# State space branch of a two-block transformer: a group's turning moved behind the norm of the group before, its features ahead of that group's second part

## The chip, the cores and the metric

The kernel runs on one core of one Trainium2 chip. The metric is the device time of one execution in microseconds (us), less is better. Engines: PE is TensorE (matmuls and transposes), PEld its weight loads, DVE is VectorE, ACT is ScalarE, POOL is GpSimd, SP is SyncE, whose queue loads the weights.

## The reference, cut to what matters

Two transformer blocks, D = 1024, 512 tokens, batch 1. The change lies in the state space branch of the second block: `proj` is the normed hidden state times `w_in`; 2048 columns `z` are the gate, 4096 columns `xbc` the features, 64 the time steps. There are 8 groups of 4 heads (head width 64), a state of 128 and 4 chunks of 128 tokens.

```python
def ssd_branch(z, xbc, dt_raw, conv_w, conv_b, dt_bias, a_log, d_skip, norm_g):
    xbc = silu(depthwise_conv_centred(xbc, conv_w, conv_b))     # 5 taps along the tokens
    xs, Bm, Cm = xbc[..., :2048], xbc[..., 2048:3072], xbc[..., 3072:]
    dt = softplus(dt_raw + dt_bias); A = -exp(a_log)
    y = ssd_chunked(xs, dt_fwd, A[0], Bm, Cm) + flip(ssd_chunked(flipped, A[1])) + d_skip * xs
    y = y * silu(z)
    yg = y.reshape(b, l, 8, 256)                                # one row per group
    return (yg * rsqrt(mean(yg * yg) + EPS)) * norm_g

def ssd_chunked(x, dt, A, Bm, Cm):          # per chunk of 128 tokens, r = 4 heads of a group
    CB = einsum(Cc, Bc);  Wd = CB * segsum_exp(dt * A)
    y_diag = einsum(Wd, x * dt)
    states = einsum(Bc, decay_states, x * dt);  prev = scan(carry * decay + states)
    return y_diag + einsum(Cc, prev, exp(a_cs))
```

Behind it `ssd @ w_ssd_branch` is summed into an accumulator.

## The kernel before, in words

Every large product is three fp32r matmuls per 128 rows of the inner dimension (`mm3`, L457 to L459: high part times high, high times low, low times high), each 128x128 by 128x512. Weights come by the SP queue into `raw` and are split into the two parts `hl` by ACT (L165) and DVE (L167). PSUM has 8 banks of 128x512: three for tiles `psm` (large products) and five for tiles `pss` (everything small).

The state space stage takes about 1313 to 1800 us of the span. A group g has these parts, methods of `Group`:
- `feats` (L1273): four `psm` tiles of 24 matmuls each (two of x features, one of B, one of C), with channels on the partitions. Each is evacuated by `conv` (L1251): ACT L1253 (centre tap), four DVE passes L1257 that read the same PSUM bank, ACT L1259 (silu). It writes `xs` (buffer "xsT", two tiles, that is one group's), `Bf` and `Cf` (two each, two groups').
- `gate` (L1286): for even g the gate's columns of two groups, four `psm` tiles, ACT L1292.
- `turn` (L1294): per chunk three transposes on PE (L1302 twice, L1303) into a `pss` bank, ACT L1304 and L1305 copy it to `x` and `Bt`. It is the last reader of `xs`, so the conv of the next group's features cannot write before it.
- `first` (L1335): PE L1343 C times B, DVE L1346 its diagonal; the steps of the states (`step`: DVE L1310, PE L1312, then ACT L1315 or DVE L1319); `decays` per chunk (POOL's DMA L1327 from `aD`, DVE L1329 and L1330, ACT L1332, DVE L1333).
- `second` (L1359): per chunk PE L1368/L1370 and L1381, DVE L1371, L1375, L1376, L1382, L1383, ACT L1384 (sum of squares).
- `third` (L1386): the norm. DVE L510, POOL L506 (power), DVE L1392 on four chunks, eight PE transposes L1394, then the split ACT L468 and DVE L469 into the operand of the output product.
- `ssd_out` (L1398, two groups) and `ssd_out_group` (L1402): the output product, DVE L625.

The framework's scheduler lists the instructions by their place in the program and by when its own simulation has them ready; on the chip every engine then runs its list in that fixed order. The loop at L1417 is what it gets.

Of the kernel before, what the change touches and what calls it, by code (L numbers as in the profile page):

```python
# [246 lines left out]
def body(ctx, tc, I, out, dbg=None, stop=None):  # L247
# [12 lines left out]
    def PM():  # L260
        return ps_m.tile([P, 512], F32, tag="m", name="psm")
# [185 lines left out]
    def uk(k):  # L447
        if k < 4:
            return UAh[:, k], UAl[:, k]
        return st["UBh"][:, k - 4], st["UBl"][:, k - 4]  # L450
# [4 lines left out]
    def mm3(ps, a, b, first, last, partial=False):  # L455

        nc.tensor.matmul(ps, a[0], b[0], start=first, stop=False, skip_group_check=partial)  # L457
        nc.tensor.matmul(ps, a[0], b[1], start=False, stop=False, skip_group_check=partial)  # L458
        nc.tensor.matmul(ps, a[1], b[0], start=False, stop=last, skip_group_check=partial)  # L459
# [137 lines left out]
    def tok2(w, src, evac, n_k=8):  # L597

        for t in range(NT):
            ps = PM()  # L600
            tk = slice(t * P, (t + 1) * P)
            for k in range(n_k):
                xh, xl = src(k)
                mm3(ps, (xh[:, tk], xl[:, tk]), w[k], k == 0, k == n_k - 1)
            evac(t, ps)
# [15 lines left out]
    def add_to(dst, ps, first):  # L621
        if first:
            nc.scalar.activation(out=dst, in_=ps, func=AF.Copy)
        else:
            nc.vector.tensor_tensor(out=dst, in0=ps, in1=dst, op=ALU.add)  # L625
# [334 lines left out]
    for j in range(4):  # L960
        heads = []
        for hh in range(2):
            hd = 2 * j + hh
            Z = wk.get("Z", 1024, 4)
            G = wk.get("G", 512, 4)
# [432 lines left out]
    def ssd_out(i):  # L1398
        for u in range(2):
            tok2(WT.get(f"so{i}{u}"), uk, lambda t, ps: add_to(acc[:, t, u * 512:(u + 1) * 512], ps, i == 0), n_k=4)  # L1400

    def ssd_out_group(g):  # L1402
        for u in range(2):
            w = WT.get(f"so3{g}{u}")
            for t in range(NT):
                ps = PM()
                tk = slice(t * P, (t + 1) * P)
                for k in range(2):
                    uh, ul = uk((2 * g + k) % 4)
                    mm3(ps, (uh[:, tk], ul[:, tk]), w[k], k == 0, k == 1)  # L1410
                add_to(acc[:, t, u * 512:(u + 1) * 512], ps, False)

    G = [Group(g) for g in range(8)]
# [3 lines left out]
    for g in range(8):  # L1417
        G[g].first()
        G[g].gate()
        G[g].second()  # L1420
        if g < 7:
            G[g + 1].feats()
        else:
            ssd_out_group(6)
        if g in (2, 4, 6):
            ssd_out(g // 2 - 1)
        if g < 7:
            G[g + 1].turn()
        G[g].third()
    ssd_out_group(7)  # L1430
    for t in range(NT):
        nc.gpsimd.dma_start(h[:, t], hD[t * P:(t + 1) * P, :])
# [238 lines left out]
def kernel_body(tc, I, out, dbg=None, stop=None):  # L1671
    with ExitStack() as ctx:
        body(ctx, tc, I, out, dbg, stop)
# [25 lines left out]
```

## Time and profile before

| | |
|---|---|
| three runs | 2581.29, 2582.27, 2585.32 us; median 2582.27 |
| profiled execution | 2581.83 us, span 2580.1 us |
| busy, share of the span | PE 97%, PEld 81%, DVE 66%, ACT 47%, POOL 7% |
| granted clock of PE, mean | 0.989 |
| HBM | 109 GB/s over the span |

The span is what the profiler recorded from the first to the last instruction; 1.7 us lie around it. A line such as `1425.25 0.66 PE L1394 MATMUL pss<-ident,h ... x2 [4.51 <-DVE h L1392]` of a timeline reads: at 1425.25 us PE began two matmuls of line 1394 that took 0.66 us; before it PE had been idle for 4.51 us, which DVE's line 1392 ended by writing `h`.

### The profile page before, as it was taken

The numbers are of one execution on the slowest core, as the hardware profiler recorded it, in microseconds if no ns is written. First come the engines' busy times: TensorE is split into PE (matmuls) and PEld (weight loads), VectorE is DVE, ScalarE is ACT, GpSimd is POOL, SyncE is SP. The second block draws the span as 40 slices with busy tenths as digits, with TensorE's granted clock in tenths as the row PEclk, the third lists the DMA queues.
The fourth block names the chain that finished last, engine by engine and source line by source line (L and its number), as shares of the span: only waits on it lengthen the run. The fifth ranks groups of instructions, "written<-read, shape, count | busy, mean of one in ns | idle before, by whom it ended". The sixth has DMA issues, their size and how long they took to land. (4 is left out here: it accounts for less than half of the span.)

```text
span 2580.1 us, 33650 instructions
## 1 busy us (share of the span) xinstructions
PE 2504.9 (97%) x12848; PEld 2088.2 (81%) x12848; DVE 1714.5 (66%) x3048; ACT 1220.2 (47%) x2181; POOL 183.5 (7%) x199
## 2 busy tenths in 40 slices
PE   8999999999999989999999999998999999999998
PEld 7888888778888768877888788787887789878877
DVE  5566567775566657577477788887555466487674
ACT  6333345443476554444356554563455436444342
POOL 1100220000201030000121100010000000100000
PEclk9999999999999989999999999998999999999999
DMA  5521235333232133453334333352221233243441
GB/s 175 162 66 61 87 115 169 125 108 129 82 96 89 63 97 113 140 179 98 102 109 125 106 104 109 104 148 77 73 67 40 84 113 123 82 147 104 141 139 58
DMA packets 202001, 278.11 MB, mean 108 GB/s; under 512 B 10800, under 2 KB 127776, under 8 KB 201840
## 3 DMA queue, kind: packets, MB, share of 16 engines
q1 hardware_dynamic: 190352, 236.29, 29.4%
q0 software_dynamic: 10192, 34.96, 5.0%
q10 hardware_dynamic: 1296, 4.72, 0.5%
q8 instruction: 101, 1.65, 0.3%
q14 instruction: 60, 0.49, 0.1%
HBM read 271.56 MB, written 9.61 MB: 109 GB/s over the span
## 5 line engine op out<-in xcount | busy, mean ns | idle before, releaser
L458 PE MATMUL psm<-XTl,hl 128*128 128x512 f32 (+1 forms) x1400 | 537.3, 384 | 7.8 <-DVE XTl L466 7.8
L457 PE MATMUL psm<-XTh,hl 128*128 128x512 f32 (+1 forms) x1400 | 534.5, 382 | 5.9 <-ACT XTh L465 5.1
L459 PE MATMUL psm<-XTh,hl 128*128 128x512 f32 (+1 forms) x1400 | 533.3, 382 | 0.0
L165 ACT ACTIVATE hl<-raw 128x1024 fp32r<-128x1024 f32 x303 | 319.3, 1056 | 313.9 <-PE psm L459 132.6
L167 DVE TENSOR_TENSOR hl<-raw,hl 128x1024 fp32r<-128x1024 f32 x287 | 352.7, 1233 | 149.0 <-ACT hl L165 147.9
L458 PEld LDWEIGHTS psm<-XTl,hl 128*128 128x128 f32 x1400 | 266.3, 190 | 56.9 <-DVE XTl L466 8.6
L457 PEld LDWEIGHTS psm<-XTh,hl 128*128 128x128 f32 x1400 | 265.9, 190 | 55.7 <-ACT XTh L465 6.1
L459 PEld LDWEIGHTS psm<-XTh,hl 128*128 128x128 f32 x1400 | 266.3, 190 | 48.5
L457 PE MATMUL psm<-hl,XTh 128*128 128x512 f32 (+1 forms) x640 | 231.1, 362 | 4.4 <-ACT XTh L465 3.3
L458 PE MATMUL psm<-hl,XTh 128*128 128x512 f32 (+1 forms) x640 | 229.9, 359 | 0.1
L459 PE MATMUL psm<-hl,XTl 128*128 128x512 f32 (+1 forms) x640 | 229.1, 358 | 0.0
L457 PE MATMUL psm<-hl,UAh 128*128 128x512 f32 x368 | 148.6, 405 | 4.9 <-DVE ACC L625 1.5
L458 PE MATMUL psm<-hl,UAh 128*128 128x512 f32 x368 | 144.9, 395 | 0.0
L459 PE MATMUL psm<-hl,UAl 128*128 128x512 f32 x368 | 143.7, 396 | 0.0
L457 PEld LDWEIGHTS psm<-hl,XTh 128*128 128x128 f32 x640 | 122.3, 191 | 21.8 <-ACT XTh L465 3.7
L458 PEld LDWEIGHTS psm<-hl,XTh 128*128 128x128 f32 x640 | 122.2, 191 | 16.6 <-issue 0.5
L459 PEld LDWEIGHTS psm<-hl,XTl 128*128 128x128 f32 x640 | 122.3, 191 | 15.9 <-issue 0.5
L671 ACT ACTIVATE WK<-psm 128x512 f32<-128x512 f32 x66 | 39.5, 598 | 160.8 <-PE psm L459 160.8
L457 PE MATMUL psm<-hl,UBh 128*128 128x512 f32 (+1 forms) x240 | 93.5, 391 | 1.1 <-ACT UBh L468 0.8
L459 PE MATMUL psm<-hl,UBl 128*128 128x512 f32 (+1 forms) x248 | 94.3, 388 | 0.0
L1257 DVE SCALAR_TENSOR_TENSOR WS<-psm,CW,WS 128x511 f32<-128x511 f32 (+1 forms) x120 | 87.5, 740 | 8.7 <-ACT WS L1253 8.4
L458 PE MATMUL psm<-hl,UBh 128*128 128x512 f32 (+1 forms) x240 | 92.2, 386 | 0.0
(481 smaller groups left out, 4839.2 us busy)
## 6 DMA issues: line engine op xcount, KB each, us to landing
raw<-in_mlp_w_down_dram SPq DMA_DIRECT2D x76, 512.0 KB, 3.3
raw<-in_mlp_w_up_dram SPq DMA_DIRECT2D x64, 512.0 KB, 3.9
raw<-in_w_in_dram SPq DMA_DIRECT2D x60, 512.0 KB, 3.7
raw<-in_w_down_dram SPq DMA_DIRECT2D x38, 512.0 KB, 3.9
WS<-aD POOLq DMA_DIRECT2D x32, 512.0 KB, 5.9
raw<-in_w_up_dram SPq DMA_DIRECT2D x32, 512.0 KB, 3.7
raw<-in_w_in_dram SPq DMA_DIRECT2D x33, 256.0 KB, 3.2
raw<-in_a_w_in_dram SPq DMA_DIRECT2D x16, 512.0 KB, 4.9
```

What stands on the lines that cost most here:

```text
L165: s.nc.scalar.activation(out=h, in_=r, func=AF.Copy)
L167: eng.tensor_tensor(out=l, in0=r, in1=h.bitcast(F32), op=ALU.subtract)
L457: nc.tensor.matmul(ps, a[0], b[0], start=first, stop=False, skip_group_check=partial)
L458: nc.tensor.matmul(ps, a[0], b[1], start=False, stop=False, skip_group_check=partial)
L459: nc.tensor.matmul(ps, a[1], b[0], start=False, stop=last, skip_group_check=partial)
L671: nc.scalar.activation(out=rl, in_=ps, func=AF.Relu)
L1257: nc.vector.scalar_tensor_tensor(out=dst[:, o0:o1], in0=ps[:, o0 + d:o1 + d], scalar=cw(j), in1=dst[:, o0:o1], op0=ALU.mult, op1=ALU.add)
```

## The change

Only the order of the calls in the loop changes. No instruction is added or removed. For group g the order was first(g), gate(g), second(g), feats(g+1), output product, turn(g+1), third(g); now it is first(g), gate(g), feats(g+1), second(g), output product, third(g), turn(g+1). In the last round `ssd_out_group(6)` stands where feats would.

```diff
@@ -1417,16 +1417,16 @@
     for g in range(8):
         G[g].first()
         G[g].gate()
-        G[g].second()
         if g < 7:
             G[g + 1].feats()
         else:
             ssd_out_group(6)
+        G[g].second()
         if g in (2, 4, 6):
             ssd_out(g // 2 - 1)
+        G[g].third()
         if g < 7:
             G[g + 1].turn()
-        G[g].third()
     ssd_out_group(7)
```

POOL's and SP's lists are the same before and after. PE, DVE and ACT differ in this stage alone. Three places, all at the passage from one group to the next. Names ending in a number are tiles: `psm_...` and `pss_...` are PSUM tiles, WS_10175 is the stage's work area, h_78 the gated outputs.

PE, from the end of group 0 to the first part of group 1. Before, the four turnings of group 1 stood further up, among the matmuls of features:

```order
L459 MATMUL psm<-XTh,hl 128x512
L1394 MATMUL pss<-ident,h 128x128 x2
L1343 MATMUL pss<-WS 128x128 x4
L1312 MATMUL pss<-WS 128x256 x2
L1394 MATMUL pss<-ident,h 128x128 x6
L457 MATMUL psm<-XTh,hl 128x512
```

Now (L1302, L1303 stand there three times in a row):

```order
L459 MATMUL psm<-XTh,hl 128x512
L1394 MATMUL pss<-ident,h 128x128 x2
L1302 MATMUL pss<-ident,WS 128x128 x2
L1303 MATMUL pss<-ident,WS 128x128
...
L1394 MATMUL pss<-ident,h 128x128 x6
L1302 MATMUL pss<-ident,WS 128x128 x2
L1303 MATMUL pss<-ident,WS 128x128
L1343 MATMUL pss<-WS 128x128 x4
L457 MATMUL psm<-XTh,hl 128x512
```

The turnings of group 1 now follow the first two transposes of the norm of group 0, and the two L1312 left the place in front of the next features.

DVE at the same place. Here psm_11171, 11140 and 11213 (before) and psm_11156, 11083 and 11114 (now) are features that wait for their conv. Before:

```order
L1257 SCALAR_TENSOR_TENSOR WS_10175<-psm_11171,CW_676,WS_10175 128x510
L1257 SCALAR_TENSOR_TENSOR WS_10175<-psm_11140,CW_676,WS_10175 128x511
L167 TENSOR_TENSOR hl_11207<-raw_11133,hl_11207 128x1024
L1330 COPY_PREDICATED WS_10175<-masks_183,WS_10175 128x512
L1257 SCALAR_TENSOR_TENSOR WS_10175<-psm_11171,CW_676,WS_10175 128x511
L1392 TENSOR_SCALAR h_78<-h_78,rr_10972 128x256 x4
```

Now:

```order
L167 TENSOR_TENSOR hl_11150<-raw_11076,hl_11150 128x1024
L1330 COPY_PREDICATED WS_10175<-masks_183,WS_10175 128x512
L510 TENSOR_SCALAR ss_10890<-ss_10890 128x4
L1392 TENSOR_SCALAR h_78<-h_78,rr_10948 128x256 x4
...
L1257 SCALAR_TENSOR_TENSOR WS_10175<-psm_11156,CW_676,WS_10175 128x510
L1257 SCALAR_TENSOR_TENSOR WS_10175<-psm_11083,CW_676,WS_10175 128x510
L1257 SCALAR_TENSOR_TENSOR WS_10175<-psm_11114,CW_676,WS_10175 128x510
...
L1333 TENSOR_TENSOR WS_10175<-WS_10175,pss_10992 128x512 x4
L167 TENSOR_TENSOR hl_11401<-raw_11081,hl_11401 128x1024
L1257 SCALAR_TENSOR_TENSOR WS_10175<-psm_11083,CW_676,WS_10175 128x510
```

The norm's L1392 lost the conv passes in front of it, and the conv of all three held tiles now stands behind it.

PE, from group 1 to group 2. Before:

```order
L1394 MATMUL pss_11303<-ident_88,h_78 128x128
L1343 MATMUL pss_11320<-WS_10175 128x128 x4
L1312 MATMUL pss_11334<-WS_10175 128x256
L1312 MATMUL pss_11338<-WS_10175 128x256
L458 MATMUL psm_11624<-XTl_81,hl_11401 128x512
```

Now:

```order
L459 MATMUL psm_11609<-XTh_80,hl_11521 128x512
L1302 MATMUL pss_11314<-ident_88,WS_10175 128x128 x2
L1303 MATMUL pss_11314<-ident_88,WS_10175 128x128
L1343 MATMUL pss_11320<-WS_10175 128x128 x4
L1312 MATMUL pss_11334<-WS_10175 128x256
L1312 MATMUL pss_11338<-WS_10175 128x256
L1312 MATMUL pss_11350<-WS_10175 128x256
L457 MATMUL psm_11640<-XTh_80,hl_11516 128x512
```

The last turning, the product of C and B and the first steps of the states of group 2 now follow each other with no large matmul between them, and a new `psm` tile begins directly behind.

## Rows read from the trace of the kernel before

**Rows 1.** The page: busy time of each engine.

```profile
PE 2504.9 (97%) x12848; PEld 2088.2 (81%) x12848; DVE 1714.5 (66%) x3048; ACT 1220.2 (47%) x2181; POOL 183.5 (7%) x199
```

**Rows 2.** A stretch of the stage: PE, PEld, DVE, ACT, POOL busy, granted clock, DMA share, GB/s.

```profile
1400.00:1450.00 50.00, 45.49 (x221) 38.51 (x220) 41.41 (x97) 26.56 (x55) 4.57 (x5) 0.93 0.36 100
```

**Rows 3.** What PE waited for, 1330 to 1810 us: total us, times, longest.

```profile
PE pss L1394 <- DVE h L1392: 8.1, 3, 4.5
PE pss L1312 <- DVE WS L1310: 3.8, 2, 2.9
PE pss L1381 <- DVE WS L1382: 3.3, 2, 2.4
PE psm L457 <- DVE WS L1257: 2.3, 2, 1.5
PE pss L1343 <- DVE WS L1246: 1.6, 1, 1.6
PE pss L1370 <- DVE WS L1319: 1.2, 1, 1.2
```

**Rows 4.** PE's timeline, group 0 to 1: start, us, instruction, [idle before].

```profile
1420.13 0.39 PE L458 MATMUL psm<-XTl,hl 128*128 128x512 f32 x1
1420.36 0.39 PE L459 MATMUL psm<-XTh,hl 128*128 128x512 f32 x1
1425.25 0.66 PE L1394 MATMUL pss<-ident,h 128*128 128x128 f32 x2 [4.51 <-DVE h L1392]
1425.71 1.91 PE L1343 MATMUL pss<-WS 128*128 128x128 f32 x8
1429.12 1.47 PE L1394 MATMUL pss<-ident,h 128*128 128x128 f32 x6
1430.26 0.56 PE L457 MATMUL psm<-XTh,hl 128*128 128x512 f32 x1
```

**Rows 5.** DVE's timeline at the same place.

```profile
1417.01 0.69 DVE L1329 TENSOR_TENSOR WS<-WS 128x512 f32<-128x512 f32 x1 [1.55 <-DMA WS<-aD]
1421.05 1.40 DVE L1257 SCALAR_TENSOR_TENSOR WS<-psm,CW,WS 128x510 f32<-128x510 f32 x2
1422.37 1.22 DVE L167 TENSOR_TENSOR hl<-raw,hl 128x1024 fp32r<-128x1024 f32 x1
1423.50 0.72 DVE L1330 COPY_PREDICATED WS<-masks,WS 128x512 f32<-128x512 uint8 x1
1424.11 0.73 DVE L1257 SCALAR_TENSOR_TENSOR WS<-psm,CW,WS 128x511 f32<-128x511 f32 x1
1424.77 1.13 DVE L1392 TENSOR_SCALAR h<-h,rr 128x256 f32<-128x256 f32 x4
1425.81 0.74 DVE L1257 SCALAR_TENSOR_TENSOR WS<-psm,CW,WS 128x511 f32<-128x511 f32 x1
```

**Rows 6.** POOL's timeline at the same place.

```profile
1421.23 1.05 POOL L506 TENSOR_TENSOR rr<-ss,mhalf 128x4 f32<-128x4 f32 x1 [1.93 <-DVE ss L510]
```

**Rows 7.** PE's timeline: group 1 to 2, and the end of group 7.

```profile
1484.59 0.75 PE L1312 MATMUL pss<-WS 128*128 128x256 f32 x2 [2.87 <-DVE WS L1310]
...
1790.67 1.94 PE L1394 MATMUL pss<-ident,h 128*128 128x128 f32 x8 [3.35 <-DVE h L1392]
```

**Rows 8.** The stretches behind the two long waits, and one behind a short one.

```profile
1425.00:1430.00 5.00, 4.75 (x19) 4.31 (x20) 5.00 (x13) 1.30 (x4) 0.00 (x0) 0.50 0.34 101
1485.00:1490.00 5.00, 5.00 (x17) 4.00 (x16) 4.93 (x14) 4.48 (x5) 0.00 (x0) 0.66 0.00 0
1590.00:1595.00 5.00, 4.43 (x20) 3.75 (x21) 5.00 (x14) 2.54 (x4) 0.00 (x0) 1.00 0.58 201
```

**Rows 9.** DVE's groups, 1330 to 1810 us: busy us, mean ns of one.

```profile
L1310 DVE TENSOR_TENSOR WS<-WS 128x256 f32<-128x256 f32 x48 | 19.5, 417 | 1.8 <-ACT WS L1304 1.7
L1346 DVE CUSTOM_DVE_ANT_0 WS<-pss,ident 128x128 f32<-128x128 f32 x32 | 9.1, 284 | 0.3
```

**Rows 10.** ACT's groups, same stretch: the first tap of conv.

```profile
L1253 ACT ACTIVATE WS<-psm,CW 128x512 f32<-128x512 f32 x29 | 22.4, 773 | 26.4 <-PE psm L459 26.3
```

## The prediction

> **What bounds the kernel now.** I read the page first: PE is busy for 97% of the span [rows 1], so time is lost or won only where PE stands still or runs at the lower clock. The changed stage is where it does: in 1400 to 1450 us PE is busy for 45.5 of 50 us at a mean granted clock of 0.93, and DVE for 41.4 [rows 2]. Then the waits of PE in the stage, 23.4 us in all, of which the rows show the large ones [rows 3]. Nearly all end with DVE. The two longest are 4.51 us of a norm's transposes for L1392 [rows 4] and 2.87 us of a state step's L1312 for L1310 [rows 7]. What change and stage share is left aside: at the start L1343 for L1246 and one L457 for L1257 of 0.8, in the last group L1381 for L1382 and L1394 for L1392, 3.35 [rows 3, 7], and 0.9 of small waits at the very end. These are 1.6 + 0.8 + 3.3 + 3.35 + 0.9 = 10.0 us; 13.4 us remain in the seven passages from a group to the next. I put them down by place: group 0 to 1 4.5, 1 to 2 4.1 (2.87 and the 1.2 of L1370), 3 to 4 0.9 (the other L1312), 4 to 5 2.0 (four small ones), 6 to 7 1.9 (one is the 1.5 of L457 for L1257), nothing at 2 to 3 and 5 to 6.
>
> The DVE timeline shows what the 4.51 consist of: L506 on POOL began at 1421.23 and took 1.05 [rows 6], so the root was there at 1422.3, but L1392 began at 1424.77, behind two L1257, a split L167, L1330 and another L1257 [rows 5]. Of 4.5 us some 2.3 are other work on DVE in front of the norm.
>
> **The change part by part.** Nothing is added or removed. The order of the lists shows that the second part was not in front of the next features in fact: in both orders these matmuls stand among group g's work, so the exchange of those two calls costs nothing by itself. What moves is turn(g+1), with what hangs on it. Its transposes are the last readers of the one pair of xsT buffers, so no conv of the features that have been computed ahead may start before it. Before, it stood in the middle of those features, and their banks were emptied while PE had large matmuls left. Now it stands behind the norm: three psm tiles are full, and that is all the banks there are, when turning, first part and conv all begin at once on DVE and ACT.
>
> Prices of one DVE row, start to start: L1257 0.66 (two from 1421.05 to 1422.37), L167 1.13, L1330 0.61, four L1392 1.04 [rows 5]; L1310 0.35 and L1346 with its short read 0.37, both near their means of 417 and 284 ns [rows 9], since rows overlap by some 0.07. L1329 and L1333 are taken as 0.6 like L1330, L469 as L1257 (same size), L1382 and L1383 as L1310. A matmul of 128x512 is 0.23 (1420.13 to 1420.36 [rows 4]).
>
> *Group 0 to 1.* First a gain: L1392 loses the conv in front. From the landing at 1417.0 [rows 5] DVE now has two L1329, two L1330, L1382, L1383 and L167: 1.2 + 1.2 + 0.7 + 1.1 = 4.2, then L510, the hand-over and 1.05 on POOL [rows 6]: L1392 can begin at about 1422.8 and not at 1424.77, 2.0 earlier. But PE reaches it earlier too, since four turnings no longer precede: six transposes take 1.14 at half clock (1429.12 to 1430.26 [rows 4]), so a turning of three 0.3 at full clock, four 1.3. The wait is 4.5 - 2.0 + 1.3 = 3.8. Next, psm_11187 needs a fourth bank. The first to come free is that of psm_11156, whose last L1257 stands eleven DVE rows after L1392 begins: 1.04 + four L1257 2.6 + two L469 1.3 + L1329, L1330 1.2 + L1310 and L1346 0.7 = 6.9, so at 1429.7. PE has till then two, twelve and six transposes and L1343 (1.70 at half clock, to the next row at 1427.41 [rows 4]): 0.5 + 2.3 + 1.1 + 1.7 = 5.6 from 1423.3 on if the clock is half, 2.8 if it is full: a wait of 0.8 to 3.6; I take 2.2. Then psm_11412 needs the bank of psm_11083: seven L1257, L1310, three L1346, four L1333 and L167, 4.6 + 0.4 + 1.1 + 2.4 + 1.1 = 9.6, against PE's 24 matmuls and two L1312, 5.9: 3.6 with rounding. Sum 9.6, where before had 4.5.
>
> *Group 1 to 2.* Directly behind the last turning PE has L1343 and three L1312. Before the first L1312, ACT passes three L1253 (0.77 each [rows 10]) and DVE four L1257, two L1346 and L1310: 2.6 + 0.7 + 0.4 = 3.7, of which L1343 hides little: 3.6. Before the next, four L1257, L1346 and L1310, 3.3 less the step's own 0.4: 2.9. The new psm tile then waits 0.4. Sum 6.9, before 4.1.
>
> *The others*, counted in the same way: 2 to 3 nothing; 3 to 4 5.6 (its output product needs banks too: 2.8 for one, 2.8 for steps behind L1257), before 0.9; 4 to 5 nothing, before 2.0; 5 to 6 3.9, before 0; 6 to 7 4.0, before 1.9. In these the split L167 of the next weights stands up to five times among the conv passes, 1.13 each [rows 5].
>
> All: 9.6 + 6.9 + 5.6 + 3.9 + 4.0 = 30.0 against 13.4, **+16.6 us**. The half clock behind the two long waits is there before (0.50 over 5 us and 0.66 over 5 us [rows 8], 2.5 + 1.7 us lost) and stays, since waits of 3.6 and more stand at the same places: nothing added. POOL's and SP's lists are unchanged, so L1327's transfers and the weights start behind the same neighbours; nothing for them.
>
> Bounds, since no row shows a conv held as a whole: the waits of L457 for L1257, which is what a missing bank costs, are 2.3 us in the whole stage before [rows 3], so the low end is that the new waits only replace old ones, +0. The high end is the longest wait, 4.5, in each of the seven passages, 31.6 - 13.4 = +18, and half clock behind three more of them at 2.1 each: +24. I stay with the count, which is nearest to the 4.51 row, as that one shows the same kind of queue on DVE.
>
> In the trace before, PE's waits for a bank are 2.3 us of 23.4 [rows 3], so banks do not bind there. A rule of the Trainium skill speaks against this change: "Perfetto Trace Analysis", section "Optimization Strategy", says that a gap repeating on the engine that should be full can mean too few buffers for the next tile. By the trace before alone the sum would be +0, by the rule repeated at each group it would be the high end; no run yet shows which.
>
> **The rivals.** *The same time* (0.15): features are ahead in both orders, and the new waits stand where DVE made PE wait anyway; for it speaks that the total DVE work is the same and that DVE has 8.6 us idle of 50 [rows 2]; against, that DVE's idle time lies elsewhere, not where three tiles are held. +0 to +5, 2582 to 2587.
>
> *Faster* (0.08), the other side: with no conv of held features in front, L1392 and L1310 come at once, and the waits of 4.51 and 2.87 [rows 4, 7] go with their half clock of 2.5 and 1.7 [rows 8]: -11.6, 2570 us. It decides at one point: the conv of the held features has to free a bank within the 24 matmuls (5.5 us) that PE should have behind the turning. The order speaks against: PE has only L1343, or nothing, there.
>
> *The clock* (0.17): the rows show 0.50 and 0.66 behind waits of 4.51 and 2.87, and 1.00 behind one of 0.9 [rows 8]. If each of the new waits of 2.3 to 3.6 us does as the 2.87 did, at three more places, 3 x 2.1 = 6.3 come on top: 2604.7 us. The Trainium skill, "TensorE: Matmul & The Clock Gate", section "HAM oscillation — how this bites in real kernels", describes a kernel that falls to the lower clock at every repeated gap; the rows agree for the two longest waits, and not for short ones.
>
> **How the numbers follow.** The profiled execution took 2581.83 us, 0.44 below the median of 2582.27, so no correction: 2581.83 + 16.6 = **2598 us**. Chances: the forecast 0.60, the clock 0.17, the same 0.15, faster 0.08. A measurement can tell 0.2%, 5.2 us. Slower by more is 0.60 + 0.17 = 0.77, within it 0.15, faster 0.08. The range takes the same, the forecast and the clock: from 2582 (+0) to 2607 (+24 and rounding); left out are the faster case and what lies above.
>
> **What would show it.** Right: in the changed kernel's waits, L457 for L1257 grows from 2.3 to above 8 us and becomes one of the largest, L1394 for L1392 stays at 6 us or more, L1312 for L1310 rises to above 6; in the PE timeline a wait of 2 to 4 us behind the L1343 of group 1; the waits of the stage sum to about 40 us (30 + 10), and outside 1330 to 1810 us nothing changes. Wrong: L457 for L1257 stays near 2 us (then banks are not short, and the time is the same or less), or L1394's wait falls below 1 us at 0 to 1 (DVE was the whole cause), or the granted clock falls below 0.9 in three or more stretches of 50 us (then the clock rival).

## The result and the profile after

The changed kernel took 2609.24 us in the median of four runs (2604.15 to 2612.22), the kernel before 2581.78 beside it (2580.08 to 2585.32): ratio 1.0103, 95% interval 1.0086 to 1.0120, that is 27 us slower. Forecast were 2598 us and a range up to 2607. The way was right, the size was not. The profiled execution of the changed kernel took 2608.07 us, its span is 2606.3, 26.2 longer than before.

The page's first line of engines, which answers to [rows 1]:

```profile
PE 2516.8 (97%) x12848; PEld 2095.9 (80%) x12848; DVE 1718.3 (66%) x3048; ACT 1207.8 (46%) x2171; POOL 184.5 (7%) x199
```

PE has the same 12848 instructions, yet it is busy for 11.9 us more. That part of the time is not waiting at all: PE worked longer at the same work. ACT has ten instructions less, all of them loads of its function tables (ACT_TABLE_LOAD, 46 where there were 56, 1.28 us each); they go with the order of ACT's list, so "no instruction is added or removed" holds for all others. The larger part of the time is in the waits, here those of the changed kernel's PE from 1330 to 1840 us (total us, times, longest), which answer to [rows 3]:

```profile
PE pss L1394 <- DVE h L1392: 8.0, 3, 3.9
PE pss L1302 <- DVE UAl L469: 6.9, 3, 3.0
PE psm L457 <- DVE WS L1257: 6.7, 4, 3.0
PE pss L1312 <- DVE WS L1310: 6.5, 6, 3.0
PE pss L1302 <- ACT WS L1305: 3.4, 1, 3.4
PE pss L1381 <- DVE WS L1382: 2.7, 1, 2.7
PE psm L457 <- DVE ACC L625: 2.6, 2, 2.3
PE pss L1343 <- DVE WS L1246: 1.6, 1, 1.6
PE pss L1370 <- DVE WS L1319: 1.4, 1, 1.4
```

With 0.6 of L457 for L468 they are 40.4 us against 23.4 before, 17.0 more. Two lines are new, and neither was named in the prediction: L1302, the first transpose of a turning, waits for L469 and for L1305. The PE timeline of the changed kernel, one line for each large wait:

```profile
1421.23 0.41 PE L1394 MATMUL pss<-ident,h 128*128 128x128 f32 x2 [3.91 <-DVE h L1392]
...
1429.20 0.80 PE L457 MATMUL psm<-XTh,hl 128*128 128x512 f32 x1 [3.04 <-DVE WS L1257]
...
1490.60 0.69 PE L1302 MATMUL pss<-ident,WS 128*128 128x128 f32 x2 [2.98 <-DVE UAl L469]
...
1496.21 2.05 PE L1312 MATMUL pss<-WS 128*128 128x256 f32 x4 [3.00 <-DVE WS L1310]
...
1607.76 0.44 PE L1302 MATMUL pss<-ident,WS 128*128 128x128 f32 x2 [2.74 <-DVE UAl L469]
...
1630.92 0.79 PE L457 MATMUL psm<-hl,UAh 128*128 128x512 f32 x1 [2.29 <-DVE ACC L625]
...
1751.04 0.77 PE L457 MATMUL psm<-hl,UAh 128*128 128x512 f32 x1 [1.78 <-DVE WS L1257]
...
1784.33 0.69 PE L1302 MATMUL pss<-ident,WS 128*128 128x128 f32 x2 [3.44 <-ACT WS L1305]
```

The reader is to see the place of the third line. At 1490.60 the fourth turning of group 2 begins, and what lets it begin is L469, the end of the split of the norm's transposes. L469 writes nothing that a turning reads; it is the last reader of the norm's two `pss` tiles. So this is a wait for a PSUM bank. What kept the bank full stands in ACT's and DVE's timelines of the changed kernel:

```profile
1486.39 1.28 ACT L1332 ACTIVATE WS<-WS 128x128 f32<-128x128 f32 x4 [6.37 <-DVE WS L1330]
1487.58 1.04 ACT L165 ACTIVATE hl<-raw 128x1024 fp32r<-128x1024 f32 x1
1488.53 1.23 ACT L468 ACTIVATE UAh<-pss,COL 128x512 fp32r<-128x512 f32 x2
```

```profile
1484.89 0.69 DVE L1329 TENSOR_TENSOR WS<-WS 128x512 f32<-128x512 f32 x1 [3.55 <-DMA WS<-aD]
...
1488.65 1.22 DVE L167 TENSOR_TENSOR hl<-raw,hl 128x1024 fp32r<-128x1024 f32 x1 [1.20 <-ACT hl L165]
1489.80 1.40 DVE L469 SCALAR_TENSOR_TENSOR UAl<-pss,COL,UAh 128x512 fp32r<-128x512 f32 x2
```

The norm's transposes had ended at 1481.8, but ACT began the split L468 of their tiles only at 1488.53. In front of it ACT's list has an L1332, for which ACT stood idle for 6.37 us: it hung on DVE's L1330 behind an L1329 that waited 3.55 us for its transfer from `aD`. Then a weight's split stands in front of the norm's on both engines, 1.04 and 1.22 us, while PE stands still. At 3 to 4 and 5 to 6, too, L468 began 7.0 and 6.2 us after the norm's transposes had ended. So the bank came free late because of what stood ahead of L468 in the lists; whether a split earlier in the list would spare the wait was not tried.

The time that PE worked longer is at the lower clock. Stretches around the large waits: PE, PEld, DVE, ACT, POOL busy, granted clock, DMA share, GB/s. The changed kernel:

```profile
1421.00:1425.00 4.00, 3.77 (x19) 3.80 (x20) 2.62 (x7) 2.54 (x8) 0.00 (x0) 0.57 0.90 211
1428.00:1436.00 8.00, 6.80 (x18) 5.36 (x19) 8.00 (x19) 3.94 (x7) 0.00 (x0) 0.57 0.00 0
1489.00:1504.00 15.00, 9.37 (x27) 7.22 (x28) 14.04 (x30) 7.21 (x17) 0.00 (x0) 0.54 0.21 65
1629.00:1637.00 8.00, 6.08 (x16) 4.81 (x17) 5.27 (x14) 0.63 (x1) 0.00 (x0) 0.57 0.21 66
1749.00:1757.00 8.00, 6.22 (x18) 4.76 (x17) 5.93 (x15) 0.63 (x1) 0.00 (x0) 0.57 0.23 66
1783.00:1791.00 8.00, 6.54 (x22) 5.34 (x23) 7.51 (x19) 4.19 (x14) 0.00 (x0) 0.57 0.44 130
1810.00:1825.00 15.00, 8.99 (x29) 7.37 (x30) 6.53 (x18) 2.79 (x8) 2.16 (x3) 0.54 0.21 71
```

The kernel before, all that it has:

```profile
1423.00:1431.00 8.00, 5.75 (x23) 5.22 (x24) 8.00 (x18) 2.62 (x7) 0.00 (x0) 0.57 0.36 98
1485.00:1489.00 4.00, 4.00 (x13) 3.16 (x12) 3.93 (x13) 3.81 (x5) 0.00 (x0) 0.57 0.00 0
1782.00:1800.00 18.00, 12.71 (x42) 10.45 (x42) 8.15 (x24) 3.19 (x10) 2.16 (x3) 0.53 0.24 83
```

What a stretch loses is its busy time times what the clock lacks to 1. In the passages that is 3.77 x 0.43 = 1.6, then 2.9, 4.3, 2.6, 2.7 and 2.8: 16.9 us in six stretches, against 2.5 + 1.7 = 4.2 in two before. The last line of each is the end of group 7, 4.1 against 6.0. Sum: passages' waits +17.6 (31.0 against 13.4), their clock +12.7, and the end of the stage -2.4 (waits and clock), together 27.9 us. The stage grew by 28.3: its last wait for L625 ended 26.1 us later (1826.69, before 1800.62), and the L458 behind the turning of group 0, where the lists are still the same, began 2.3 us earlier (1362.15, before 1364.41), which has nothing to do with the change.

### The profile page after: what moved, and what is told of

It reads as the page before. It is cut to its first block, busy times and chain, and to the rows that moved or that the text cites. A ratio compares the mean times of both kernels' runs of the same rounds, so it can differ in the third digit from the quotient of the medians.

```text
span 2606.3 us, 33635 instructions
## 1 busy us (share of the span) xinstructions
PE 2516.8 (97%) x12848; PEld 2095.9 (80%) x12848; DVE 1718.3 (66%) x3048; ACT 1207.8 (46%) x2171; POOL 184.5 (7%) x199
## 3 DMA queue, kind: packets, MB, share of 16 engines
q1 hardware_dynamic: 190352, 236.29, 28.3%
## 5 line engine op out<-in xcount | busy, mean ns | idle before, releaser
L457 PE MATMUL psm<-XTh,hl 128*128 128x512 f32 (+1 forms) x1400 | 536.4, 384 | 10.1 <-ACT XTh L465 5.1
L458 PE MATMUL psm<-XTl,hl 128*128 128x512 f32 (+1 forms) x1400 | 535.7, 383 | 7.8 <-DVE XTl L466 7.8
L167 DVE TENSOR_TENSOR hl<-raw,hl 128x1024 fp32r<-128x1024 f32 x287 | 353.0, 1234 | 140.4 <-ACT hl L165 139.3
L457 PEld LDWEIGHTS psm<-XTh,hl 128*128 128x128 f32 x1400 | 266.4, 191 | 60.5 <-ACT XTh L465 6.1
L458 PEld LDWEIGHTS psm<-XTl,hl 128*128 128x128 f32 x1400 | 266.9, 191 | 57.6 <-DVE XTl L466 8.6
L457 PE MATMUL psm<-hl,XTh 128*128 128x512 f32 (+1 forms) x640 | 231.0, 361 | 1.7 <-DVE ACC L625 0.9
L458 PE MATMUL psm<-hl,XTh 128*128 128x512 f32 (+1 forms) x640 | 230.0, 360 | 0.3 <-DVE hl L172 0.3
L457 PE MATMUL psm<-hl,UAh 128*128 128x512 f32 x368 | 150.7, 410 | 5.8 <-DVE ACC L625 2.6
L458 PE MATMUL psm<-hl,UAh 128*128 128x512 f32 x368 | 147.6, 402 | 0.0
L457 PEld LDWEIGHTS psm<-hl,XTh 128*128 128x128 f32 x640 | 122.2, 191 | 19.3 <-DVE ACC L625 1.1
L458 PEld LDWEIGHTS psm<-hl,XTh 128*128 128x128 f32 x640 | 122.2, 191 | 16.8 <-DVE hl L172 0.6
L457 PE MATMUL psm<-hl,UBh 128*128 128x512 f32 (+1 forms) x240 | 94.2, 394 | 1.1 <-ACT UBh L468 0.8
L458 PE MATMUL psm<-hl,UBh 128*128 128x512 f32 (+1 forms) x240 | 92.6, 387 | 0.0
L1257 DVE SCALAR_TENSOR_TENSOR WS<-psm,CW,WS 128x510 f32<-128x510 f32 (+1 forms) x120 | 86.7, 743 | 9.0 <-ACT WS L1253 8.8
```

Of the source, the lines that this page charges most:

```text
L167: eng.tensor_tensor(out=l, in0=r, in1=h.bitcast(F32), op=ALU.subtract)
L1257: nc.vector.scalar_tensor_tensor(out=dst[:, o0:o1], in0=ps[:, o0 + d:o1 + d], scalar=cw(j), in1=dst[:, o0:o1], op0=ALU.mult, op1=ALU.add)
```

## The experiments

After the result there were two theories. A: the conv of the features ahead is held by the pair of `xsT` buffers, as the prediction had it. B: the turning and the norm want PSUM banks at the same time, four and two `pss` tiles where five exist. Every run was timed beside the kernel before, on the same chip.

**Which half of the change.** First the exchange of `second` and `feats` without the move of the turning:

```diff
-        G[g].second()
         if g < 7:
             G[g + 1].feats()
         else:
             ssd_out_group(6)
+        G[g].second()
```

> Only the exchange of second and feats; turning stays in front of third. Theory A (what costs is the turning behind the norm, because it holds the conv of the features ahead): the instruction lists are those of the kernel before up to group 3, so 2579 to 2585 us, PE waits of the stage near 23 us. Rival C (the exchange costs by itself): a third or more of the 27 us, 2590 us or above.

2584.09 us against 2583.44, ratio 1.0002 (0.9993 to 1.0012): no difference. Then the turning alone:

```diff
-        if g < 7:
-            G[g + 1].turn()
         G[g].third()
+        if g < 7:
+            G[g + 1].turn()
```

> Only the turning moved behind the norm; second stays in front of feats as before. The lists of all engines are the same, row for row, as those of the changed kernel, so every theory that gives the exchange of second and feats no part says the time of the changed kernel, 2604 to 2612 us.

2609.41 us against 2584.48, ratio 1.0097 (1.0080 to 1.0114), the time of the changed kernel. The lists are the changed kernel's, so the whole effect is the turning's place; the exchange costs nothing that can be measured.

**The xsT buffers.** In the changed kernel:

```diff
-            s.xs = [wk.get("xsT", 512, 2) for n in range(2)]
+            s.xs = [wk.get("xsT", 512, 4) for n in range(2)]
```

> The changed kernel with four xsT buffers instead of two, so that the conv of the next features need not wait for the turning. Theory A (the hold of the conv): the 31 us of waits in the seven passages fall to about 10 to 15 and the 17 us lost at half clock to 5 or less, 2578 to 2588 us. Rival B (the turning's place by itself: its PSUM banks and the chain norm, turning, first part): the waits of L1302 (10.3 us) stay, and 2598 us or above.

2606.31 us against 2583.44, ratio 1.0087 (1.0072 to 1.0102). Theory A falls: with the hold gone the time stays within 3 us of the changed kernel's, and L457 waits 6.5 us for conv where it waited 6.7. But B was not right in detail either. The L1302 waits shrank from 10.3 to 0.4 us, so the two holds are not independent; other waits came in their place. The largest is 10.9 us of L1394 at 6 to 7, here with DVE's timeline of that run around its end:

```profile
1778.87 0.66 PE L1394 MATMUL pss<-ident,h 128*128 128x128 f32 x2 [10.91 <-DVE h L1392]
```

```profile
1777.77 0.69 DVE L1329 TENSOR_TENSOR WS<-WS 128x512 f32<-128x512 f32 x1 [2.31 <-DMA WS<-aD]
1778.38 1.14 DVE L1392 TENSOR_SCALAR h<-h,rr 128x256 f32<-128x256 f32 x4
```

The norm's root was there at 1776.3 (POOL's L506 began at 1775.12 and took 1.21), but L1392 stood behind an L1329 that waited for its transfer from `aD`. That is some 2 of the 10.9 us. Before it, the last pieces of `second` on DVE had stood behind two more L1329, which waited 1.87 and 0.72 us for theirs, and two L167. DVE's list is fixed, so the norm waited for data that it does not use. This run alone decides nothing between B and a third cause.

**The number of banks.** The turning packed, still behind the norm: the x of two chunks in one bank, all of Bt in one, three `pss` tiles instead of four, and three copies on ACT instead of eight:

```diff
-            for c in range(4):
-                ps = PS()
...
+            for cc in range(2):
+                ps = PS()
+                for c in range(2 * cc, 2 * cc + 2):
...
+                nc.scalar.activation(out=s.x[:, 2 * cc:2 * cc + 2], in_=ps.rearrange("p (c n) -> p c n", c=2), func=AF.Copy)
+            ps = PS()
...
+            nc.scalar.activation(out=s.Bt, in_=ps.rearrange("p (c n) -> p c n", c=4), func=AF.Copy)
```

> The changed kernel with the turning packed into three pss banks instead of four (x of two chunks in one, all of Bt in one; 3 copies on ACT instead of 8). Theory A: the conv stays held, so the waits of L457 and L1312 stay; only the L1302 waits for L469 (6.9 us) can go, and the clock behind them; 2598 to 2606 us. Rival B: the banks of the turning are the larger part, 2590 us or below.

2589.06 us against 2583.44, ratio 1.0019 (1.0010 to 1.0029): of the 27 us, some 20 are gone. The waits of PE in that run (its norm is five lines lower, L1399 is the norm's transpose, L1348 the product of C and B):

```profile
PE pss L1399 <- DVE h L1397: 9.9, 3, 5.6
PE psm L457 <- DVE ACC L625: 4.1, 5, 1.5
PE pss L1348 <- ACT WS L1305: 3.7, 1, 3.7
...
PE pss L1348 <- DVE UAl L469: 2.2, 1, 2.2
PE psm L457 <- DVE WS L1257: 2.2, 1, 2.2
```

No turning waits any more. The wait for a bank is still there at two passages, 2.2 and 3.7 us, but of the next tile, L1348's. In all, PE's waits fell from 40.4 to 29.2 us: those for a `pss` bank from 10.3 to 5.9, L457's for conv from 6.7 to 2.2, the states' L1312 for L1310 from 6.5 to 1.7 (L1317 and L1315 there). So less than half of it is the wait for the bank itself; with the packing the order of the lists changed as well. Two controls had to follow: that packing does not help by itself, and that it is the banks and not the copies.

> The control for the packed turning: the same packing in the kernel before. Theory B (the turning behind the norm needs four pss banks beside the norm's two, six where there are five; packed it needs five): before, the turning is done before the norm's banks are taken, so packing gives nothing there, 2579 to 2586 us. Rival D (packing is faster wherever it stands, through 3 copies on ACT instead of 8): as much as the 20 us between the changed kernel and its packed form, 2563 to 2570 us.

The kernel before with the same packing: 2583.79 us against 2583.62, ratio 1.0000 (0.9991 to 1.0009). So packing is worth nothing in time where the turning stands ahead of the norm.

> The changed kernel with the turning in three pss banks, but with its 8 copies on ACT as before. Theory B (banks): 2585 to 2594 us, as the packed one with 3 copies; the L1302 waits for L469 stay away. Rival D (the copies): back to 2600 us or more.

Three banks, but each chunk copied by itself as in the changed kernel: 2588.69 us against 2583.62, ratio 1.0021 (1.0012 to 1.0031). The copies are worth nothing.

Then the count of banks was put back to four. The first attempt filled and copied Bt chunk by chunk in two banks:

```diff
-            ps = PS()
             for c in range(4):
+                ps = PS() if c % 2 == 0 else ps
...
-            for c in range(4):
-                nc.scalar.activation(out=s.Bt[:, c], in_=ps[:, c * P:(c + 1) * P], func=AF.Copy)
+                nc.scalar.activation(out=s.Bt[:, c], in_=ps[:, tk], func=AF.Copy)
```

> The changed kernel with the turning packed by two chunks but in four pss banks again (x in two, Bt in two), with 8 copies on ACT. Theory B (the number of banks): with the norm's two that is six again where there are five, so the wait for L469 returns: 2600 to 2610 us, as the changed kernel. Rival E (the order of transposes and copies, not the banks): 2585 to 2594 us, as with three banks.

2617.43 us against 2584.48, ratio 1.0131 (1.0116 to 1.0146), above what either theory said. It had a fault as a test: the second transpose into a bank waited for the copy out of the first, 5.4 us in its waits, and its norm waited 18.7 us for L1398, 11.2 of them at one place. So the same again, with the transposes ahead of the copies; against the text of the run with three banks and eight copies this differs in nothing but the tile that Bt's last two chunks go to, and what the scheduler makes of it:

```diff
-            ps = PS()
+            pb = [PS(), PS()]
...
-                nc.tensor.transpose(ps[:, tk], s.Bf[:, tk], ident)
+                nc.tensor.transpose(pb[c // 2][:, tk], s.Bf[:, tk], ident)
...
-                nc.scalar.activation(out=s.Bt[:, c], in_=ps[:, c * P:(c + 1) * P], func=AF.Copy)
+                nc.scalar.activation(out=s.Bt[:, c], in_=pb[c // 2][:, c * P:(c + 1) * P], func=AF.Copy)
```

> The packed turning with 8 copies, changed in one thing: Bt's four transposes go into two pss banks of two and not into one of four, and their copies follow all of them, so that no transpose waits for a copy out of its own bank, as it did in the run before this. Theory B (the number of banks): six wanted where there are five, 2600 to 2612 us, with waits of PE for L469 or for copies of the turning of 5 us or more in all. Rival E (what the run before this added was the interleaving of transposes and copies): 2585 to 2594 us, as with three banks.

2600.68 us against 2583.30, ratio 1.0060 (1.0047 to 1.0074): one bank more costs 12 us (2588.69 with three). The waits of PE in that run (L1310 is Bt's transpose, L1306 a copy of x):

```profile
PE psm L457 <- DVE WS L1257: 7.1, 4, 2.5
PE pss L1310 <- ACT WS L1306: 5.9, 3, 3.5
...
PE pss L1310 <- DVE UAl L469: 2.4, 2, 2.2
```

The transposes into the sixth tile wait 8.3 us for the copies and splits that free a bank, as L1302 did in the changed kernel (10.3), and L457's wait for conv is back at 7.1. So a tile more at this place takes back 12 of the 20 us that packing gave, which speaks for theory B. That all 12 are the wait for the bank is not shown: beside the run with three banks and eight copies, the waits for a `pss` bank rose from 5.3 to 8.3 us only, L457's for conv from 1.8 to 7.1, and the lists of PE, DVE and ACT differ from group 0 on. What the new order does by itself no run held apart. The other 8, between this run and the changed kernel, go with how four banks are filled; what of it does it was not tried.

**Both holds lifted.**

> The changed kernel with the packed turning and four xsT buffers: both holds lifted. If the xsT hold costs something of its own beside the banks, 2575 to 2585 us, below the packed one alone (2589). If lifting it only lets conv stand in front of the norm again, as the run with four buffers alone suggests (a wait of 10.9 us of L1394 there), 2589 us or above.

The packed turning and four xsT buffers: 2588.03 us against 2583.62, ratio 1.0017 (1.0009 to 1.0026), 1 us below packing alone, less than a measurement can tell. The xsT hold costs nothing beside the banks. The numbers lie between the two expectations, nearer to the second.

**The turning moved the other way**, ahead of second:

```diff
+        if g < 7:
+            G[g + 1].turn()
         G[g].second()
...
-        if g < 7:
-            G[g + 1].turn()
         G[g].third()
```

> The turning moved the other way: first, gate, feats of the next group, turn of the next group, second, output product, third. Theory A: nothing is held, the norm's L1394 stands behind 32 more large matmuls and finds L1392 done; the 13.4 us of waits in the passages of the kernel before fall below 5 and with them its 4.3 us at half clock: 2565 to 2575 us. Rival B: since the turning then does not follow the norm either, the same sign, but the second part's DVE work is pushed behind conv, L1370 and L1381 wait in its place: 2578 us or above.

2612.44 us against 2583.44, ratio 1.0110 (1.0094 to 1.0125). A's expectation failed by some 40 us. B's number, 2578 or above, has no upper end and so holds, but B said the same sign as A, and the waits of L1370 and L1381 that it named did not come. The waits of PE there:

```profile
PE pss L1394 <- DVE h L1392: 13.3, 3, 8.1
PE psm L457 <- DVE WS L1257: 13.0, 6, 3.6
PE psm L457 <- DVE ACC L625: 8.2, 3, 4.8
```

Conv has its data earlier, yet the psm waits for it are the longest of all runs, and the norm waits longer too. Why its DVE list came out so was not followed up. What it shows is that the place before is better than the new one and than this one too.

**The clock.** In the kernel before, 24 transposes without use were put between L1381 and L1394 of the last group, a place where that leaves the lists of PE, DVE and ACT as they were, but for two small DVE instructions that changed places with L1392:

```diff
-            pts = [PS(), PS()]
+            pts = [PS(), PS()]; [nc.tensor.transpose(pts[i // 4 % 2][:, i % 4 * P:(i % 4 + 1) * P], s.ab[3][:, i % 2 * P:(i % 2 + 1) * P], ident) for i in range(24 if g == 7 else 0)]
```

> The kernel before with 24 idle transposes (of a chunk's product, overwritten by the norm's own) between L1381 and L1394 of the last group, where PE stands idle for 3.35 us, about 0.14 us each. Theory of the clock (a PE that stands still for about 3 us comes back at half clock, and that is where the 13 us beside the waits come from): in this last stretch the loss at half clock falls from 5.9 us to 2 to 4, and the time by 2 to 4 us, to 2578 to 2580 us, though work was added. Rival (the clock falls for another reason): the loss stays near 5.9 us and the time is the same or up to 1 us longer.

2582.59 us against 2583.62, ratio 0.9997 (0.9988 to 1.0006): no difference that can be measured. The 2 to 4 us that the theory of the clock said did not come; what the stretch loses at half clock fell from 6.0 us to 4.4 (9.36 x 0.47), where it said 2 to 4 and the rival 5.9. So as a time it decides nothing. Its PE timeline and stretch:

```profile
1791.71 5.38 PE L1390 MATMUL pss<-ident,WS 128*128 128x128 f32 x24 [0.52 <-DVE WS L1382]
1796.89 1.25 PE L1394 MATMUL pss<-ident,h 128*128 128x128 f32 x8
1798.80 0.50 PE L457 MATMUL psm<-hl,UAh 128*128 128x512 f32 x1 [0.67 <-ACT UAh L468]
1799.14 0.40 PE L458 MATMUL psm<-hl,UAh 128*128 128x512 f32 x1
1799.38 0.40 PE L457 MATMUL psm<-hl,UAh 128*128 128x512 f32 x1
```

```profile
1787.00:1798.00 11.00, 9.36 (x46) 8.88 (x45) 5.63 (x18) 1.93 (x8) 1.01 (x2) 0.53 0.03 8
1798.00:1805.00 7.00, 6.00 (x26) 4.53 (x25) 3.29 (x5) 1.27 (x2) 1.15 (x2) 1.00 0.42 150
```

PE came into the fill already at half clock, from the L1381 waits in front, so 24 transposes took 5.2 us, where the expectation had 24 x 0.14 = 3.4, and reached past the wait of 3.35. But behind them the output product ran at full clock from its second matmul on (0.24 from start to start), where the kernel before, after its idle wait, ran its first thirteen matmuls at about 0.43. Counted from the first of the L1381 waits' ends, full clock was back after 11.4 us (1786.56 to 1798), in the kernel before after 16.4 (1782.52 to 1798.88), and a later L457 that waits for L625 began 17.0 us after it where it had been 18.1. So at this place a busy PE got its clock back earlier than an idle one, for 1.1 us, read from one profiled execution of each; at the passages the same is read from the rows and was not tried.

No run was faster than the kernel before, and none points to one that would be.

## Why the prediction was right or wrong

*What moves.* Right: the exchange costs nothing (2584.09 against 2583.44), the turning is all.

*The waits.* The sum was right and its parts were not. Forecast for the passages were 30.0 us, measured are 31.0. By passage, forecast and then measured: 0 to 1 9.6 and 6.95 (3.91 + 3.04), 1 to 2 6.9 and 7.7, 3 to 4 5.6 and 6.95, 4 to 5 none in both, 5 to 6 3.9 and 4.6, 6 to 7 4.0 and 4.8. The norm's wait at 0 to 1 came out at 3.91 for 3.8, and L457 behind L1343 at 3.04 for a range of 0.8 to 3.6. The wait of psm_11412, 3.6, did not come; PE had stood longer at the wait before it and went through the matmuls between at half clock (0.57 in 1428 to 1436), which gave conv the time. In its place came 10.3 us of L1302 that the count had no term for; that the sum agrees all the same is luck. The prediction looked at the three psm banks only. It counted the turning's transposes (four at 0.3 are 1.2, not 1.3, which changes nothing) but not the tiles they go to: the order that it quoted shows the norm's two `pss` tiles open around three turnings, which is all five banks, with a fourth turning to come.

*The signs.* Of the signs of being right these came: L1394 8.0 us for 6 or more, L1312 6.5 for above 6, a wait of 3.04 behind the L1343 of group 1, and 40.4 for about 40 in all. L457 for L1257 came to 6.7 and not above 8. The sign of the clock rival nearly came: of the stretches of 50 us from 1400 to 1850 two had a granted clock below 0.9 (0.87 and 0.86) and two had 0.90, where before one had 0.83 and all others 0.93 or more.

*The hold by xsT*, given as the mechanism, was not what cost: four buffers changed the time by 3 us, and by 1 us beside the packed turning. It bears on the L1302 waits, which went with four buffers, but other waits then took their time.

*The clock.* This is the step that failed: "nothing added", because the long waits stood at the same places as before. Measured are 16.9 us at half clock against 4.2, so +12.7; with the forecast's 2598 that is 2611, where 2609 was measured. The clock rival was the right one, but too small: three more stretches of 2.1, where four more came and those that were there before grew, 1489 to 1504 alone to 4.3. The prediction also called 4.51 and 2.87 the two longest waits; the 3.35 of the last group is longer than the second, and 0.53 stands in the stretch around it (1782 to 1800). It treated a passage's waits as one; two waits close together, as 2.98 and 3.00 at 1 to 2, keep PE at half clock through the work between.

The Trainium skill, "TensorE: Matmul & The Clock Gate", section "HAM oscillation — how this bites in real kernels", has a kernel that falls to the lower clock at every repeated gap. The trace agrees in six stretches at 0.54 to 0.57 behind the waits of the passages, but not behind the wait of 2.74 us at 1607.76, around which the clock was 1.00. The Trainium skill, "Perfetto Trace Analysis", section "Optimization Strategy", says that a repeating gap can mean too few buffers for the next tile. The trace agrees for `pss` banks: L1302 waited for one at four of the seven passages, and one tile less at this place took 12 us less.

*The faster rival* had its condition answered by the trace: a bank would have had to come free within the 24 matmuls behind the turning, and PE waited 3.04 us for it at once.

## What to carry to other kernels

When a step is moved, count the PSUM tiles that are open at its new place, pool by pool, against the pool's banks: a step that needs four beside another's two in a pool of five can wait for the slowest reader of the other, whatever its own inputs do. Then look at what stands ahead of that reader in its engine's list. Price a new wait of the engine that bounds the kernel twice, once for itself and once for the slower clock behind it; here 17.6 us of waits came with 12.7 us of half clock. A list that is fixed in advance makes the norm wait for a neighbour's transfer or split that it does not read, so look at what stands in front, not only at what is waited for.

## What the runs showed of the hardware that was not expected

Short waits were followed by the lower clock too: 2.29 us (1630.92) and 1.78 us (1751.04) of the changed kernel, with smaller ones of 0.4 to 1.2 us in the microseconds before, have 0.57 around them, while 0.9 us of the kernel before had 1.00 [rows 8]. A longer wait, the 2.74 us at 1607.76, was not followed by it:

```profile
1606.00:1614.00 8.00, 6.24 (x33) 5.40 (x34) 5.95 (x13) 6.49 (x16) 0.00 (x0) 1.00 0.43 131
```

So in these runs the length of one wait does not tell by itself whether the clock falls, and a price for the clock per wait is an average. Filling a wait of PE was worth nothing that can be measured where PE entered it at half clock already: 24 transposes took 5.2 us there, and the time did not move.
